# Block 2's projections on two alternating sets of PSUM banks, with the heads' norm sums after the next projection

## The chip, the cores and the metric

The kernel runs on one core of one Trainium2 chip. The metric is device time in microseconds (us) of one execution; lower is better.

## What is computed

Two transformer blocks on 512 tokens of width 1024, in float32. Block 1 is attention with a pooling mixer and a gated convolutional FFN. Block 2, which the change touches, starts with one wide projection, from which a neighbourhood attention and a two-way gated delta net are fed; a mixture of experts follows. The part of the reference that matters, cut:

```python
h = rms_norm(x, ln1_g)
proj = h @ w_in                          # (512, 3600)
aq, ak, av, dqkv, dz, dab = jnp.split(proj, [...], axis=-1)
aq = rms_norm(hs(aq), q_norm_g)          # per head of 64
ak = rms_norm(hs(ak), k_norm_g)
attn = rms_norm(neighbourhood_attention(aq, ak, hs(av), rpb), attn_out_g)
dn = bidirectional_gated_deltanet(dqkv, dz, dab[:, :, 0], dab[:, :, 1], conv_w, a_log, dt_bias, dn_out_g)
x = x + jnp.concatenate([attn, dn], axis=-1) @ w_out
x = x + hierarchical_moe(rms_norm(x, ln2_g), ...)
```

In the delta net q, k and v pass a depthwise convolution of width 5 and a SiLU; each chunk of its keys gives a triangular system that is solved.

## The kernel before

Every large product is made of float32 numbers split in two parts: `split_w` (L156) loads half a weight piece, ACT rounds it to `whi` (L170) and DVE makes the rest `wlo` (L171), each with three buffers. `proj` (L181) makes 256 output columns of all 512 tokens: two accumulators of 128 x 512, each one PSUM bank, and 3 x 8 matmuls for each (`mm3`, L177 to L179), 48 in all. The banks have tags (L102): `mm`, `pa` and `pb` have two each, `pc` and `gv` one.

```python
banks = dict(mm=2, pa=2, pb=2, pc=1, gv=1)
def proj(src, hh, hl, tag="mm", n=8):
```

In block 1's FFN the projections already take turns between tags (L619, L640). In block 2 all of them use `mm`, so the first matmul of one waits until ACT or DVE has read the banks of the one before. The value projections `na_v` make four tiles, one bank each, in turn in the two `mm` banks.

The stage is written in this order (L1208 to L1245): `na_q(0)`, the projection of the attention's keys, `na_v(0)`, `dn_k(0)`, `dn_k(1)`, `na_q(1)` (called q1 here), the keys' second projection (k1), `dn_q(1)`, `dn_q(0)`, `na_v(1)`, `substitute`, `dn_v(1)`, `dn_v(0)`, `dn_z(0)`, `dn_z(1)`, then `levels`, `scan_prep`, `na_pairs` and the scans. Each tile's waits are found by a planner, which also gives every engine a fixed queue: it goes by this order, but takes a later instruction when an earlier one isn't ready by its own estimate. A buffer or bank is given back when its last reader has run. Each engine works through its queue in order.

What the prediction follows:

- `head_norm` (L723): for each half of a projection ACT makes a gained copy `a` (L729) and a square `sq` (L732), both from the six buffers of tag `cv`; PE sums the squares of each head (`hn`, L735, 8 small matmuls for a half) into a `pa` bank; DVE (L739, L740, L743) and POOL (L742) make reciprocal roots. `head_rows` (L747) turns them into rows (`hr`, L750, a `pa` bank), which DVE copies to `hrow` (L752) and a DMA writes to `hscr` (L754). `head_bcast` (L757) reads them back into `hR`, and `na_q_out`, `na_k_out` (L769, L774) multiply the gained copies with them and thereby give these back.
- `conv_silu` (L863): ACT copies a projection's half out of its bank (`cn`, L866), POOL scales it (L867), ACT, DVE and ACT make the convolution and tanh (L868 to L874), DVE the result (L875). It holds two `cv` buffers from L866 to L875.
- `dn_k_out` (L957): for each head PE turns the keys (`ktr`, L961) and multiplies them (`kk`, L981), both in the one `gv` bank; `decay` (L942) makes E by DVE and ACT (L948), DVE makes U (L987), and DMAs write it out for `substitute`.
- `substitute` (L1004): 31 steps on DVE and POOL side by side (L1016, L1018) that need U of all four heads. `levels` (L1076) reads its result; its first matmuls are `lvY`.
- `na_pairs` (L796): the attention's logits `nS` (L812) go into `pa` banks, which DVE reads (L816); its sums `npo` use `pc`.

Of the kernel before, what the change touches and what calls it, by code (L numbers as in the profile page):

```python
# [14 lines left out]
AF = mybir.ActivationFunctionType  # L15
# [74 lines left out]
def hybrid_kernel(ctx, tc, A, out, dbg=None):  # L90
# [14 lines left out]
    def ps(tag, name):  # L105
        return pp.tile([128, 512], F32, tag=tag, name=name, bufs=banks[tag])
# [613 lines left out]
    nc.gpsimd.memset(vsh[0][0:64], 0.0)  # L720
    nc.gpsimd.memset(vsh[4][64:128], 0.0)

    def head_norm(pp, gain):  # L723

        pt = ps("pa", "hn")
        aa = []
        for m in range(2):
            a = slot("cv", "a", 6)
            nc.scalar.activation(a, pp[m], AF.Copy, scale=gain)  # L729
            aa.append(a)  # L730
            sq = slot("cv", "sq", 6)
            nc.scalar.activation(sq, pp[m], AF.Square)  # L732
            for t in range(4):
                o = m * 8 + t * 2
                nc.tensor.matmul(pt[:, o:o + 2], sq[:, t * 128:t * 128 + 128], C("hsel"), start=True, stop=True)  # L735
        v, r = (sp_.tile([128, 2] + d, F32, tag=f"hn{i}", name="hnv", bufs=1 + i) for i, d in enumerate(([4, 2], [2, 4])))
        pv = pt[:, 0:16].rearrange("p (m t e) -> p m t e", m=2, t=4)
        for m in range(2):
            nc.vector.tensor_tensor(v[:, m], pv[:, m], rr2.unsqueeze(2).to_broadcast([128, 4, 2]), op=ALU.mult)  # L739
        nc.vector.tensor_scalar(v, v, 1.0 / 64, EPS, op0=ALU.mult, op1=ALU.add)  # L740
        for m in range(2):
            nc.gpsimd.tensor_tensor(v[:, m], v[:, m], nhalf.rearrange("p (t e) -> p t e", t=4), op=ALU.pow)  # L742
            nc.vector.tensor_tensor(r[:, m].rearrange("p e t -> p t e"), v[:, m], rr.unsqueeze(2).to_broadcast([128, 4, 2]),  # L743
                                    op=ALU.mult)
        return aa, r

    def head_rows(aa, r):  # L747

        pr = ps("pa", "hr")
        nc.tensor.transpose(pr[0:16, 0:128], r.rearrange("p m e t -> p (m e t)"), ident)  # L750
        row = tmp("hrow")[0:16, 0:128]
        nc.vector.tensor_copy(row, pr[0:16, 0:128])  # L752
        hscr = drp.tile([2, 2, S], F32, tag="hscr", name="hscr", bufs=4)
        nc.sync.dma_start(hscr.rearrange("m e (t p) -> (m e t) p", t=4), row)  # L754
        return aa, hscr

    def head_bcast(hscr, m):  # L757
# [2 lines left out]
            nc.sync.dma_start(R[64 * e:64 * e + 64], hscr[m, e:e + 1].to_broadcast([64, S]))  # L760
        return R

    def na_q(c):
        return head_norm(proj(A["win2"][c] if c else w_first, hh, hl), g8)

    def na_q_out(c, aa, r):
        for m in range(2):
# [10 lines left out]
    def na_v(c):  # L778
        w = 256 if c else 272
        hi, lo = split_w(A["win2"][5] if c else A["win2v"], w=w)  # L780
        for i in range(4):
            p = ps("mm", "pv")
            ts = slice(i * 128, i * 128 + 128)
            for k in range(8):
                mm3(p[:, 0:w], hh[k][:, ts], hl[k][:, ts], hi[k], lo[k], k, k == 0, k == 7)
            if not c:
                nc.vector.tensor_scalar(dab[:, i, :], p[:, 256:272], rr[:, i:i + 1], None, op0=ALU.mult)
            v = slot("nP", "vn", 4, (128, 256))
            nc.scalar.activation(v, p[:, 0:256], AF.Copy, scale=rr[:, i:i + 1])
            nc.sync.dma_start(vscr[c][ts], v)  # L790
        src = vscr[c].rearrange("(r b x) w -> b r x w", r=8, b=8)
        for b in range(8):
            i, o = (b + 1) // 2, 64 * ((b + 1) % 2)
            nc.sync.dma_start(vsh[i][o:o + 64, c * 256:c * 256 + 256], src[b])
# [154 lines left out]
        E[d, h] = e  # L949

    def dn_k(c):
        p = proj(A["win2"][6 + c], hh, hl)
        for m in range(2):
            h = 2 * c + m
            conv_silu(p[m], 4 + h, kT[h])
# [66 lines left out]
                nc.sync.dma_start(xblk[d, h].rearrange("t b r c -> (t b) r c"), XB[i:i + 16])  # L1022

    def dn_q(c):
        p = proj(A["win2"][8 + c], hh, hl)
        for m in range(2):
            h = 2 * c + m
            conv_silu(p[m], h, qT[h])
# [11 lines left out]
    vT = {}  # L1040

    def dn_v(c):
        p = proj(A["win2"][10 + c], hh, hl)
        for m in range(2):
            h = 2 * c + m
            vT[h] = tmp("vT")
            conv_silu(p[m], 8 + h, vT[h])
# [12 lines left out]
    zs = []  # L1060

    def dn_z(c):
        p = proj(A["win2"][12 + c], hh, hl)
        z = slot("Z", "zs", 2, (128, 2, S))
        for m in range(2):
            zs.append(z[:, m])
            a = tmp("za")
            nc.vector.scalar_tensor_tensor(a, p[m], 0.5, RR, op0=ALU.mult, op1=ALU.mult)
            t = tmp("zt")
            nc.scalar.activation(t, a, AF.Tanh)  # L1070
            nc.vector.scalar_tensor_tensor(zs[2 * c + m], t, 1.0, a, op0=ALU.add, op1=ALU.mult)
# [135 lines left out]

    q_ = na_q(0)  # L1208
    x_rows(2)
    pk = proj(A["win2"][2], hh, hl)  # L1210
    x_rows(0)
    k_ = head_norm(pk, V("kg"))
    q_ = head_rows(*q_)
    na_v(0)
    x_rows(3)
    x_rows(1)
    na_q_out(0, *q_)
# [8 lines left out]
    na_k_out(0, *k_)  # L1226
    dn_k_out(0)
    q2_ = na_q(1)
    pk2 = proj(A["win2"][3], hh, hl)
    dn_k_out(1)  # L1230
    q2_ = head_rows(*q2_)
    na_q_out(1, *q2_)
    k2_ = head_norm(pk2, V("kg"))
    k2_ = head_rows(*k2_)
    na_k_out(1, *k2_)
    dn_q(1)
# [615 lines left out]
```

## Time and profile before

| | |
|---|---|
| median of three runs | 1566.13 us (1556.18 to 1568.72) |
| the profiled execution | 1565.13 us, span 1563.3 us |
| PE (TensorE) busy | 1472.4 us, 94% of the span |
| DVE (VectorE) busy | 835.6 us, 53% |
| ACT (ScalarE) busy | 516.3 us, 33% |
| POOL (GpSimd) busy | 248.3 us, 16% |
| mean granted TensorE clock | 0.969 |

All times of the trace are us from the start of the span. Block 2's projections run from about 625 to 856, the levels and scans to about 1000, the experts from 1074 to the end. A row of the timeline gives start, duration, engine, line, operation, output and inputs, how many instructions it merges, and in brackets how long the engine had been idle before and what ended that. Matmul ends are modelled and overlap the next starts. A clock of 1.00 is 2.4 GHz, and a mean between 0.50 and 1.00 in a stretch is a mix of 2.4 and 1.2 GHz.

### The profile page before, as it was taken

Reading aid. Unit: us, or ns where it says so; the run is one execution under the profiler, and the core shown is the slowest. Engines: PE = TensorE matmul, PEld = TensorE weight load, DVE = VectorE, ACT = ScalarE, POOL = GpSimd, SP = SyncE. Lnnn points to the kernel's source line nnn. Section 1 sums busy time; section 2 is a strip of 40 time slices with the busy share of each in tenths; the row PEclk is TensorE's granted clock in tenths of the full one; section 3 lists DMA queues with packets and bytes.
Section 4 is the critical chain, followed back from the end, with each engine's and each line's share of the span. In section 5 each row is a group of like instructions: output and inputs, shape, how many; then the busy total and the mean of one; then the engine's idle time right before and its main releaser. Section 6 shows DMA issues by size and latency. Waiting matters only on the chain.

```text
span 1563.3 us, 20383 instructions
## 1 busy us (share of the span) xinstructions
PE 1472.4 (94%) x7501; PEld 1009.8 (65%) x7501; DVE 835.6 (53%) x1665; ACT 516.3 (33%) x981; POOL 248.3 (16%) x314
## 2 busy tenths in 40 slices
PE   6989999999999999898889999997999999999997
PEld 2756687788888887786667788894444444444443
DVE  3669777654565467357797666635333333333234
ACT  3444434442333245354334444422311111111111
POOL 0234011000000003314471331102110000000000
PEclk8979999999999999998989999997999999999999
DMA  8664142322223223344243131567999999999995
GB/s 305 224 214 135 60 144 72 131 94 95 94 96 98 94 90 95 100 148 134 71 133 79 29 85 55 183 230 279 419 417 421 422 421 421 421 421 421 420 420 191
DMA packets 82573, 327.69 MB, mean 210 GB/s; under 512 B 18086, under 2 KB 21798, under 8 KB 58144
## 3 DMA queue, kind: packets, MB, share of 16 engines
q1 hardware_dynamic: 80736, 321.63, 55.3%
q0 software_dynamic: 1728, 4.66, 0.8%
q8 instruction: 61, 1.00, 0.3%
q14 instruction: 48, 0.39, 0.1%
HBM read 319.42 MB, written 8.47 MB: 210 GB/s over the span
## 4 chain that ended last, share of the span: by engine, by line
PE 75%; DVE 9%; DMA 6%; POOL 3%; issue 3%; ACT 3%; SPq 1%; DVEq 0%; POOLq 0%; ACTq 0%
PE pgu L1662 14%; PE pj L177 10%; PE pj L179 10%; PE pj L178 10%; PE pd L1691 7%; DMA graw<-in_modw_dram 3%; PE pkept L1709 2%; PE pkept L1710 2%; PE pcmb L1709 2%; PE pcmb L1710 2%; DVE wlo L171 1%; DVE cv L872 1%; DMA xg<-xs,tok_of 1%; PE pS L482 1%; PE po L178 1%
## 5 line engine op out<-in xcount | busy, mean ns | idle before, releaser
L177 PE MATMUL pj<-hh,whi 128*128 128x512 f32 x640 | 260.9, 409 | 18.7 <-ACT cn L866 8.5
L179 PE MATMUL pj<-hh,wlo 128*128 128x512 f32 x640 | 257.7, 404 | 2.4 <-DVE wlo L171 2.4
L178 PE MATMUL pj<-hl,whi 128*128 128x512 f32 x640 | 257.7, 403 | 0.6 <-DVE hl L200 0.6
L1662 PE MATMUL pgu<-wgu,xw 128*64 128x512 f32 x1024 | 226.8, 595 | 0.1
L171 DVE TENSOR_TENSOR wlo<-wraw,whi 128x1024 fp32r<-128x1024 f32 (+4 forms) x126 | 151.2, 1201 | 51.3 <-ACT whi L170 48.1
L170 ACT ACTIVATE whi<-wraw 128x1024 fp32r<-128x1024 f32 (+4 forms) x126 | 129.1, 1027 | 137.6 <-PE pj L178 115.8
L1662 PEld LDWEIGHTS pgu<-wgu,xw 128*64 128x64 f32 x1024 | 70.7, 137 | 139.0 <-issue 137.0
L177 PEld LDWEIGHTS pj<-hh,whi 128*128 128x128 f32 x640 | 123.9, 194 | 53.5 <-ACT cn L866 11.4
L179 PEld LDWEIGHTS pj<-hh,wlo 128*128 128x128 f32 x640 | 123.9, 194 | 32.6 <-issue 4.0
L178 PEld LDWEIGHTS pj<-hl,whi 128*128 128x128 f32 x640 | 123.9, 194 | 28.2 <-issue 2.1
L1668 DVE SCALAR_TENSOR_TENSOR hid<-pgu,agt,sg 128x256 f32<-128x256 f32 x32 | 15.5, 484 | 194.6 <-ACT sg L1666 194.6
L1666 ACT ACTIVATE sg<-pgu,agt 128x256 f32<-128x256 f32 x32 | 15.2, 474 | 306.9 <-PE pgu L1662 306.9
L1691 PE MATMUL pd<-wd,hT 128*64 128x512 f32 x512 | 115.5, 593 | 0.1
L1713 DVE TENSOR_TENSOR xr<-xr,pcmb 128x512 f32<-128x512 f32 x128 | 82.2, 683 | 30.3 <-PE pcmb L1710 30.3
L304 POOL TENSOR_TENSOR acc<-acc,sq 128x512 f32<-128x512 f32 x21 | 33.7, 1622 | 390.5 <-ACT sq L303 390.2
L198 DVE SCALAR_TENSOR_TENSOR og<-pd,agt,og 128x512 fp32r<-128x512 f32 x64 | 48.0, 751 | 79.5 <-ACT og L194 79.5
L1653 POOL COPY xw<-xgT 128x512 f32 x56 | 32.8, 614 | 356.0 <-PE pgu L1662 345.7
L1691 PEld LDWEIGHTS pd<-wd,hT 128*64 128x64 f32 x512 | 36.4, 137 | 71.9 <-issue 62.9
L179 PE MATMUL pj<-ah,wlo 128*128 128x512 f32 x176 | 69.3, 394 | 0.0
L177 PE MATMUL pj<-ah,whi 128*128 128x512 f32 x176 | 69.3, 394 | 0.0
L178 PE MATMUL pj<-al,whi 128*128 128x512 f32 x176 | 69.3, 394 | 0.0
L194 ACT ACTIVATE og<-pd,agt 128x512 fp32r<-128x512 f32 x64 | 44.0, 687 | 75.3 <-PE pd L1691 74.3
(454 smaller groups left out, 2607.1 us busy)
## 6 DMA issues: line engine op xcount, KB each, us to landing
wgu<-in_egu_dram SPq DMA_DIRECT2D x128, 1024.0 KB
wd<-in_ed_dram SPq DMA_DIRECT2D x62, 1024.0 KB
graw<-in_modw_dram SPq DMA_DIRECT2D x48, 512.0 KB
wraw<-in_wup_dram SPq DMA_DIRECT2D x42, 512.0 KB
wraw<-in_win_dram SPq DMA_DIRECT2D x38, 512.0 KB
wraw<-in_wdn_dram SPq DMA_DIRECT2D x20, 512.0 KB
wraw<-in_wout_dram SPq DMA_DIRECT2D x16, 512.0 KB
E<-gscr SPq DMA_DIRECT2D x16, 256.0 KB
```

Of the source, the lines that this page charges most:

```text
L170: nc.scalar.activation(hi, raw, AF.Copy)
L171: nc.vector.tensor_tensor(lo, raw, hi.bitcast(F32), op=ALU.subtract)
L177: nc.tensor.matmul(p, whi, hh, start=first, stop=False)
L178: nc.tensor.matmul(p, whi, hl, start=False, stop=False)
L179: nc.tensor.matmul(p, wlo, hh, start=False, stop=last)
L194: nc.scalar.activation(hi, src, AF.Identity, scale=scale, bias=0.0 if bias is None else bias)
L198: nc.vector.scalar_tensor_tensor(lo, src, scale, hi.bitcast(F32), op0=ALU.mult, op1=ALU.subtract)
L1662: nc.tensor.matmul(gu[64 * i:64 * i + 64, :], xw[:, j, 64 * i:64 * i + 64], wts.gu[e][j], start=(j == 0), stop=(j == 7))
L1691: nc.tensor.matmul(pd[64 * i:64 * i + 64, :], hT[:, j, 64 * i:64 * i + 64], wts.d[e][:, j, n * 512:n * 512 + 512], start=(j == 0), stop=(j ...
L1709: nc.tensor.matmul(pc, OT[:, ts], a, start=(n == 1 or start), stop=False, skip_group_check=(n == 0))
L1710: nc.tensor.matmul(pc, OT[:, ts], b, start=False, stop=(n == 1 or stop), skip_group_check=(n == 0))
L1713: nc.vector.tensor_tensor(v, v, pc, op=ALU.add)
```

## The change

Each projection of block 2 is given a tag, `mm` or `pa`, by a table `PJ`; consecutive ones differ, and the four value tiles alternate. `head_norm` is cut in two: `head_copies` makes the squares and gained copies (squares first) right behind the projection, and `head_norm` makes the sums later, behind the next projection (for the first keys: behind the value projection). Sums and rows move from `pa` to the single `pc` bank. The rows of the first q are made behind `na_v(0)` now.

```diff
--- before.py
+++ after.py
@@ -720,19 +720,23 @@
     nc.gpsimd.memset(vsh[0][0:64], 0.0)
     nc.gpsimd.memset(vsh[4][64:128], 0.0)
 
-    def head_norm(pp, gain):
-
-        pt = ps("pa", "hn")
-        aa = []
+    def head_copies(pp, gain):
+
+        aa, sqs = [], []
         for m in range(2):
-            a = slot("cv", "a", 6)
-            nc.scalar.activation(a, pp[m], AF.Copy, scale=gain)
-            aa.append(a)
-            sq = slot("cv", "sq", 6)
-            nc.scalar.activation(sq, pp[m], AF.Square)
+            sqs.append(slot("cv", "sq", 6))
+            nc.scalar.activation(sqs[m], pp[m], AF.Square)
+            aa.append(slot("cv", "a", 6))
+            nc.scalar.activation(aa[m], pp[m], AF.Copy, scale=gain)
+        return aa, sqs
+
+    def head_norm(aa, sqs):
+
+        pt = ps("pc", "hn")
+        for m in range(2):
             for t in range(4):
                 o = m * 8 + t * 2
-                nc.tensor.matmul(pt[:, o:o + 2], sq[:, t * 128:t * 128 + 128], C("hsel"), start=True, stop=True)
+                nc.tensor.matmul(pt[:, o:o + 2], sqs[m][:, t * 128:t * 128 + 128], C("hsel"), start=True, stop=True)
         v, r = (sp_.tile([128, 2] + d, F32, tag=f"hn{i}", name="hnv", bufs=1 + i) for i, d in enumerate(([4, 2], [2, 4])))
         pv = pt[:, 0:16].rearrange("p (m t e) -> p m t e", m=2, t=4)
         for m in range(2):
@@ -746,7 +750,7 @@
 
     def head_rows(aa, r):
 
-        pr = ps("pa", "hr")
+        pr = ps("pc", "hr")
         nc.tensor.transpose(pr[0:16, 0:128], r.rearrange("p m e t -> p (m e t)"), ident)
         row = tmp("hrow")[0:16, 0:128]
         nc.vector.tensor_copy(row, pr[0:16, 0:128])
@@ -760,8 +764,15 @@
             nc.sync.dma_start(R[64 * e:64 * e + 64], hscr[m, e:e + 1].to_broadcast([64, S]))
         return R
 
+
+    PJ = dict(q0="mm", k0="pa", v=("mm", "pa", "mm", "pa"), dk0="mm", dk1="pa", q1="mm", k1="pa", dq1="mm", dq0="pa",
+              dv1="mm", dv0="pa", dz0="mm", dz1="pa")
+
     def na_q(c):
-        return head_norm(proj(A["win2"][c] if c else w_first, hh, hl), g8)
+        return head_copies(proj(A["win2"][c] if c else w_first, hh, hl, tag=PJ[f"q{c}"]), g8)
+
+    def na_k(c):
+        return head_copies(proj(A["win2"][2 + c], hh, hl, tag=PJ[f"k{c}"]), V("kg"))
 
     def na_q_out(c, aa, r):
         for m in range(2):
@@ -779,7 +790,7 @@
         w = 256 if c else 272
         hi, lo = split_w(A["win2"][5] if c else A["win2v"], w=w)
         for i in range(4):
-            p = ps("mm", "pv")
+            p = ps(PJ["v"][i], "pv")
             ts = slice(i * 128, i * 128 + 128)
             for k in range(8):
                 mm3(p[:, 0:w], hh[k][:, ts], hl[k][:, ts], hi[k], lo[k], k, k == 0, k == 7)
@@ -949,7 +960,7 @@
         E[d, h] = e
 
     def dn_k(c):
-        p = proj(A["win2"][6 + c], hh, hl)
+        p = proj(A["win2"][6 + c], hh, hl, tag=PJ[f"dk{c}"])
         for m in range(2):
             h = 2 * c + m
             conv_silu(p[m], 4 + h, kT[h])
@@ -1022,7 +1033,7 @@
                 nc.sync.dma_start(xblk[d, h].rearrange("t b r c -> (t b) r c"), XB[i:i + 16])
 
     def dn_q(c):
-        p = proj(A["win2"][8 + c], hh, hl)
+        p = proj(A["win2"][8 + c], hh, hl, tag=PJ[f"dq{c}"])
         for m in range(2):
             h = 2 * c + m
             conv_silu(p[m], h, qT[h])
@@ -1040,7 +1051,7 @@
     vT = {}
 
     def dn_v(c):
-        p = proj(A["win2"][10 + c], hh, hl)
+        p = proj(A["win2"][10 + c], hh, hl, tag=PJ[f"dv{c}"])
         for m in range(2):
             h = 2 * c + m
             vT[h] = tmp("vT")
@@ -1060,7 +1071,7 @@
     zs = []
 
     def dn_z(c):
-        p = proj(A["win2"][12 + c], hh, hl)
+        p = proj(A["win2"][12 + c], hh, hl, tag=PJ[f"dz{c}"])
         z = slot("Z", "zs", 2, (128, 2, S))
         for m in range(2):
             zs.append(z[:, m])
@@ -1207,11 +1218,12 @@
 
     q_ = na_q(0)
     x_rows(2)
-    pk = proj(A["win2"][2], hh, hl)
+    k_ = na_k(0)
     x_rows(0)
-    k_ = head_norm(pk, V("kg"))
+    q_ = head_norm(*q_)
+    na_v(0)
     q_ = head_rows(*q_)
-    na_v(0)
+    k_ = head_norm(*k_)
     x_rows(3)
     x_rows(1)
     na_q_out(0, *q_)
@@ -1226,11 +1238,12 @@
     na_k_out(0, *k_)
     dn_k_out(0)
     q2_ = na_q(1)
-    pk2 = proj(A["win2"][3], hh, hl)
+    k2_ = na_k(1)
+    q2_ = head_norm(*q2_)
     dn_k_out(1)
     q2_ = head_rows(*q2_)
     na_q_out(1, *q2_)
-    k2_ = head_norm(pk2, V("kg"))
+    k2_ = head_norm(*k2_)
     k2_ = head_rows(*k2_)
     na_k_out(1, *k2_)
     dn_q(1)
```

## Rows read from the trace of the kernel before

**Rows 1.** Stretches: length; PE, PEld, DVE, ACT, POOL busy us (instructions); clock; DMA share; GB/s.

```profile
700.00:720.00 20.00, 14.35 (x68) 11.35 (x67) 19.57 (x33) 8.71 (x20) 10.80 (x9) 1.00 0.55 157
720.00:740.00 20.00, 18.81 (x77) 15.57 (x77) 11.99 (x39) 8.32 (x20) 6.84 (x13) 0.75 0.47 119
...
760.00:780.00 20.00, 14.46 (x70) 11.49 (x69) 15.34 (x41) 7.96 (x18) 8.06 (x21) 0.91 0.29 72
780.00:800.00 20.00, 14.34 (x94) 12.56 (x94) 17.14 (x33) 6.97 (x12) 17.88 (x30) 0.87 0.38 107
800.00:820.00 20.00, 17.55 (x68) 13.52 (x69) 19.41 (x45) 7.18 (x13) 12.80 (x18) 0.87 0.47 143
820.00:840.00 20.00, 18.37 (x83) 14.59 (x82) 19.98 (x46) 8.51 (x13) 4.38 (x5) 1.00 0.23 59
```

**Rows 2.** Whom PE waited for, 640 to 856: total us, times, longest.

```profile
PE pj L177 <- ACT cn L866: 8.5, 6, 4.5
PE hn L735 <- ACT sq L732: 5.6, 2, 5.2
PE pj L177 <- ACT vn L789: 2.9, 1, 2.9
...
PE pv L177 <- ACT cn L866: 1.7, 2, 0.9
...
PE pv L177 <- ACT vn L789: 1.5, 2, 0.9
```

**Rows 3.** A stretch of the FFN in block 1; columns as in rows 1.

```profile
300.00:360.00 60.00, 60.00 (x265) 49.42 (x264) 35.54 (x43) 24.62 (x32) 0.00 (x0) 1.00 0.31 99
```

**Rows 4.** PE in order of time, around k1.

```profile
720.84 1.87 PE L735 MATMUL hn<-cst,sq 128*128 128x2 f32 x8 [5.17 <-ACT sq L732]
...
729.97 0.67 PE L961 MATMUL ktr<-cst,kT 128*128 128x128 f32 x4
```

**Rows 5.** DVE in order of time, keys and substitution.

```profile
722.41 1.13 DVE L987 SCALAR_TENSOR_TENSOR U<-kk,nbrk,E 128x128 f32<-128x128 f32 x4
...
743.26 0.24 DVE L739 TENSOR_TENSOR hnv<-hn,rr 128x8 f32<-128x8 f32 x2 [3.90 <-PE hn L735]
743.42 1.12 DVE L987 SCALAR_TENSOR_TENSOR U<-kk,nbrk,E 128x128 f32<-128x128 f32 x4
...
771.73 0.24 DVE L752 COPY hrow<-hr 16x128 f32<-16x128 f32 x1
...
801.81 0.41 DVE L816 CUSTOM_DVE_ANT_0 nP<-nS,bm 128x256 f32<-128x256 f32 x1
...
836.54 0.15 DVE L1018 TENSOR_TENSOR XB<-XB,TB 128x8 f32<-128x8 f32 x1
```

**Rows 6.** ACT in order of time.

```profile
741.01 0.65 ACT L948 ACTIVATE E<-E 128x512 f32<-128x512 f32 x1
...
755.82 0.60 ACT L866 ACTIVATE cn<-pj 128x512 f32<-128x512 f32 x1 [1.71 <-PE pj L179]
...
767.48 0.60 ACT L866 ACTIVATE cn<-pj 128x512 f32<-128x512 f32 x1 [1.13 <-DVE qT L875]
```

**Rows 7.** PE in order of time, rows, logits, levels.

```profile
739.38 0.27 PE L750 MATMUL hr<-cst,hnv 128*16 128x128 f32 x1
...
775.16 0.70 PE L812 MATMUL nS<-akp,zq 64*128 64x256 f32 x2
...
855.99 1.06 PE L1095 MATMUL lvY<-DD,U 128*128 128x128 f32 x8
```

**Rows 8.** POOL in order of time, the substitution's start.

```profile
777.96 0.24 POOL L1016 TENSOR_TENSOR TB<-LB,XB 128x23 f32<-128x23 f32 x1
```

**Rows 9.** SyncE's queue, the first q's rows.

```profile
663.13 0.40 SPq L754 DMA_DIRECT2D hscr<-hrow  x1
...
686.90 2.43 SPq L760 DMA_DIRECT2D hR<-hscr  x4
```

**Rows 10.** PE's largest group from 1075: busy, mean ns, idle before.

```profile
L1662 PE MATMUL pgu<-wgu,xw 128*64 128x512 f32 x1022 | 226.3, 595 | 0.1
```

## Prediction

> **What bounds the kernel now.** The page's line of engines, in the table of time and profile above, comes first: PE has by far the largest share, so PE time saved is kernel time unless something else bounds the stretch where it is saved. Next the table of stretches for block 2's projections [rows 1]. Two things are to be seen in it: PE idles (14.35 us busy of 20 at 700, 14.46 at 760, 14.34 at 780), and its granted clock falls to 0.75, 0.91, 0.87 and 0.87 during or after such idleness; and VectorE (DVE) is full from 700 to 720 (19.57 of 20) and from 780 to 840 (17.14, 19.41, 19.98). So PE does not bound this stage alone. Third, whom PE waits for from 640 to 856 [rows 2]: ScalarE (ACT) copies that read a projection out of its banks: cn 8.5, sq 5.6, vn 2.9, and for the value projections 1.7 and 1.5, together 20.2 us. Fourth, a stage that already alternates its banks, the up projections of block 1's FFN [rows 3]: PE is busy 60.00 of 60 at clock 1.00, but DVE only 35.54 of 60. Last, PE, DVE and ACT in order of time, for what follows each wait [rows 4 to 8].
>
> **The change part by part.** *Banks.* No matmul is added or removed. Each projection gets another pair of banks than the one before it, so its first matmuls need not wait for that one's copies. On PE alone this removes at most the 20.2 us of [rows 2] and, with the idleness, the slow clock: (1-0.75) x 20 + (1-0.91) x 20 + 2 x (1-0.87) x 20 = 12.0 us [rows 1]. Upper bound 32.2 us; lower bound nothing, since the same copies can hold up something else.
>
> *What of it reaches the end.* The stage ends in a chain through the keys of the delta net's four heads: transposes ktr, copies, decay E, U (L987), the next head; then substitute, which needs every U; then levels. All heads' ktr and kk share the one gv bank, so head 1's ktr waits for head 0's last U, at 722.41 + 1.13 = 723.54 [rows 5]. It ran at 729.97 [rows 4]: on PE it stood behind q1's norm sums, which had waited 5.17 us for the squares, and behind the first matmuls of k1's projection at the slow clock. With k1's projection in its own banks and the sums behind it, PE goes straight on from 720.84 - 5.17 = 715.67 and can take ktr when the bank is free: 729.97 - 723.54 = 6.4 us. This is the main term. It is 0 if the new order puts another wait in front, and no more than 6.4, because U sets it.
>
> *The second wait on the chain.* Between two parts of head 1's U, DVE stood 3.90 us at hnv, for k1's norm sums [rows 5]. These now come 5.2 us of stall and some of the 5.0 us of slow clock earlier, so DVE should find them done. But U also needs its E from ACT, done at 741.01 + 0.65 = 741.66 [rows 6]: of the 3.90 us, 743.42 - 741.66 = 1.8 us are sure, and 3.4 us if ACT, which copied k1 ahead of that E, is free some 1.6 us earlier as well. I take 2.5, between the two.
>
> *After 778.* The substitution starts at 777.96 [rows 8], directly behind the last U, and its last step is at 836.54, 58.6 us later [rows 5]. From 780 to 840 DVE is busy 56.5 us of 60 [rows 1], so the end moves with the start and by no more than 3.5 us beyond it. I take 0: with more work ready at once, DVE fills, it doesn't shorten. The levels' first matmul, at 855.99 [rows 7], moves with it; PE, which ends its last projection just before, has more to spare than DVE.
>
> *Norm sums and squares.* The sums are only moved. A projection's two squares now stay in two of the six cv buffers until its sums have run, one projection later. So k1's second pair of copies waits for q1's sums (1.87 us for eight at the slow clock [rows 4]), which frees k1's banks some 2 us late, behind the next projection's 48 matmuls (48 x 60/265 = 10.9 us [rows 3]). They hide it: 0, and 2 us without them. Squares ahead of gained copies let sums start a copy earlier, which nothing waits for: 0. Pair 0's rows of q are now made behind the value projection: PE's one hr, DVE's hrow and SyncE's write of hscr pass that projection and its writes and reads on SyncE. That write was at 663.13, and the rows are read back at 686.90 [rows 9]; 23.4 us of slack hide the move, and behind them it would cost its own 0.40 us. POOL's powers move with the sums; POOL is busy 6.84 and 8.06 of 20 us at 720 and 760 [rows 1]: 0.
>
> *Sum.* 6.4 + 2.5 + 0 = 8.9 us. The profiled execution took 1565.13 us (span 1563.3 and 1.8 around it): 1565.1 - 8.9 = 1556.2. The median of the three runs lies 1.0 above that execution, within their spread of 12.5; I say 1556. The gain passes through to the end, as all that follows hangs on the levels and the experts' PE, once it runs, waits 0.1 us in 1022 matmuls [rows 10].
>
> **Two rules of the Trainium skill.** The FFN's alternating banks show a full PE [rows 3], block 2 shows 20.2 us of waits for banks [rows 2]. "Perfetto Trace Analysis", section Matmuls, says that independent groups of matmuls should rotate through different PSUM banks, so that one's evacuation overlaps the next one's matmuls; by that alone the sum would be the whole upper bound (the first rival). Against it speaks the same page's section Identifying the Most-Contended Engine: the engine with the highest occupancy is the one to improve. By that rule, from 780 on this is DVE and the change gives nothing. This trace agrees there, with 19.98 of 20, and not from 720 to 740, where DVE is busy 11.99.
>
> **The rivals.** *The banks give nearly everything.* For: the FFN's row; and DVE idles 8.0 us at 720 and 4.7 at 760 [rows 1], so it could take work earlier. Against: from 780 on it has 3.5 to give. PE's idle time at 700 and 760 goes (5.65 + 5.54 us), with the clock's loss at 720 and 760 (5.0 + 1.8), and 3.5 later: 21.5 us, 1544. The floor is 1565.1 - 32.2 = 1533.
>
> *DVE bounds it, no gain.* PE's stalls are hidden, because the copies that end them wait for buffers and not for banks. For: the copy at 767.48 waited for DVE's qT [rows 6], as gained copies of q1 and k1 hold four of the six cv buffers until their rows come back. Against: at 720 DVE itself waited, for PE. Then 1565, with DVE's slack of 3.5 to either side.
>
> *Slower: one bank for all norm sums.* The rows hr of q1 are turned at 739.38 [rows 7], but DVE copies them out only at 771.73 [rows 5]. Two pa banks let k1's sums pass them. In the single bank pc, if q1's hr gets in before k1's sums, these wait until 771.73 + 0.24 = 771.97; their squares keep two cv buffers, the gained copies four, and the next projection's first copy, today at 755.82 [rows 6], waits that long: 16.2 us on the convolutions, 1581. What decides is whether k1's squares are ready before q1's rows. The rows came 739.38 - 722.71 = 17 us after q1's first sums [rows 4, 7], the squares need only k1's last matmuls and copies of some 0.6 us each; so I hold it unlikely.
>
> *The logits keep the projections' banks.* The attention's first logits nS were issued at 775.16 [rows 7] into both pa banks, and DVE reads the first at 801.81 [rows 5], 26.7 us later. If that falls where projections want pa, PE has one projection of 10.9 us on the other set to put there: 15.8 us lost against 8.9 won, 1572.
>
> **How the numbers follow.** A measurement of this kernel can tell about 1% (15.7 us) from no change. Chances: the forecast 0.42, the banks give nearly everything 0.25, no gain 0.15, the logits 0.10, the single bank 0.08. A planner makes the order of the queues anew, which spreads each case by some us. The range 1538 to 1576 leaves out the single bank (0.08) and the lowest part of the first rival (about 0.10). The forecast's own range, each term between its bounds (0 to 6.4, 0 to 3.4, 0 to 3.5), is 1552 to 1565. Faster by over 1% (under 1549.5): the first rival and an edge of the forecast, 0.27. Slower by over 1%: the single bank and an edge of the logits, 0.10. Within 1%: 0.63.
>
> **What would show it.** Right: no wait of projections for cn, sq or vn above 1 us; head 1's ktr some 6 us nearer to q1's end; the clock near 1.00 where it was 0.75; the substitution starting near 769 and still about 58 us long; levels near 847. Wrong: a substitution much shorter than 58 us (the first rival), one that starts at 778 (no gain), k1's sums behind hrow (the single bank), or PE waiting at pj or pv for DVE's read of nS (the logits).

## The result, and the profile after

The changed kernel takes 1586.62 us (median of 4 runs, 1582.30 to 1590.90) against 1564.35 us beside it: a ratio of 1.014 [1.0111, 1.017], slower. The forecast was 1556.0 with a range of 1538 to 1576. The profiled execution took 1585.91 us, its span 1584.1.

One point before the rows are compared. Block 1 is the same code in both kernels, but its length differs from one execution to the next: the first matmul of row broadcasts (rb) in block 2's start, which the change doesn't touch, stands at 641.05 in the profile of before and at 634.91 in that of after. Below, "+x" is a time counted from that matmul in its own trace. So counted, the attention's last product (npo) ends at +351.2 before and at +376.6 after, and from there to the end it is 571 us in one and 573 in the other: nearly all that is lost is lost in these 370 us. So counted, equal code repeats closely: the first eight copies cn of before, e14 and e15 (two kernels of the experiments, whose code is that of before up to there) lie within 0.2 us of each other.

The stretches of after, with the columns of [rows 1]:

```profile
700.00:720.00 20.00, 16.00 (x72) 13.28 (x71) 17.78 (x39) 10.08 (x23) 6.87 (x16) 0.93 0.37 129
720.00:740.00 20.00, 17.80 (x92) 14.65 (x92) 11.13 (x47) 8.62 (x21) 7.88 (x14) 0.98 0.47 126
740.00:760.00 20.00, 17.46 (x87) 14.60 (x85) 13.10 (x43) 6.99 (x16) 4.49 (x18) 0.95 0.24 62
760.00:780.00 20.00, 12.37 (x66) 11.63 (x66) 9.82 (x21) 4.26 (x7) 12.20 (x15) 0.67 0.34 107
780.00:800.00 20.00, 9.90 (x47) 9.27 (x46) 9.62 (x15) 6.17 (x10) 18.12 (x29) 0.67 0.11 31
800.00:820.00 20.00, 19.04 (x70) 15.24 (x71) 15.08 (x36) 5.19 (x7) 7.32 (x12) 0.77 0.39 131
820.00:840.00 20.00, 19.15 (x84) 15.20 (x82) 18.06 (x38) 8.84 (x12) 5.39 (x3) 1.00 0.17 53
```

The stretch at 720 has a clock of 0.98 where it was 0.75, but it is not the same work: rb stands 6.14 us earlier in after. Counted from rb, the 20 us of before from 720 belong to these of after:

```profile
713.86:733.86 20.00, 15.42 (x76) 12.99 (x77) 12.17 (x44) 9.54 (x20) 7.66 (x17) 0.91 0.50 139
```

So the clock is better there, 0.91, and not full. And from 760 to 800 PE is busy 12.37 and 9.90 us of 20 at clock 0.67, and DVE, which was busy 17.14 of 20 at 780 [rows 1], is busy 9.62. Now PE, DVE and ACT idle together, which points to a chain that runs from queue to queue.

Whom PE waited for in after, 640 to 863 (total us, times, longest), against [rows 2]:

```profile
PE pv L177 <- ACT cn L877: 9.8, 2, 5.2
PE pqs L1047 <- ACT sq L1044: 4.9, 1, 4.9
PE hr L754 <- DVE hnv L747: 4.7, 2, 2.4
PE ktr L972 <- DVE U L998: 4.0, 1, 4.0
...
PE hn L739 <- DVE hrow L756: 2.5, 1, 2.5
```

No projection pj waits for a copy of cn or vn any more, and no sum hn for sq; the change does what it says. The value projection waits instead (pv for cn, 9.8 us where it was 1.7), and there is a short new wait, hn for hrow. It is only 2.5 us long, and it is the cause. PE, then ACT (k1's squares, sq, and what follows), in order of time:

```profile
725.87 1.84 PE L739 MATMUL hn<-cst,sq 128*128 128x2 f32 x16
731.87 0.27 PE L754 MATMUL hr<-cst,hnv 128*16 128x128 f32 x1 [2.20 <-DVE hnv L747]
757.49 2.97 PE L739 MATMUL hn<-cst,sq 128*128 128x2 f32 x16 [2.54 <-DVE hrow L756]
```

```profile
726.86 0.60 ACT L728 ACTIVATE sq<-pj 128x512 f32<-128x512 f32 x1 [0.30 <-PE hn L739]
...
758.78 0.60 ACT L877 ACTIVATE cn<-pj 128x512 f32<-128x512 f32 x1 [3.42 <-PE hn L739]
...
768.62 0.47 ACT L800 ACTIVATE vn<-pv,rr 128x256 f32<-128x256 f32 x1 [7.08 <-PE pv L179]
...
786.21 0.72 ACT L879 ACTIVATE cv<-cn,dcw 128x512 f32<-128x512 f32 x1 [8.62 <-POOL cn L878]
```

k1's squares are ready at 726.86 + 0.60 = 727.46. Their sums run at 757.49, 30 us later: q1's rows (hr, 731.87) were put into the single pc bank first, and DVE copies them out of it only at 757.19. The first copy of the next convolution (cn) waits for those sums, at 758.78, or +123.9; in [rows 6] it stood at 755.82, +114.8. DVE, POOL and SyncE show the rest:

```profile
755.40 1.12 DVE L998 SCALAR_TENSOR_TENSOR U<-kk,nbrk,E 128x128 f32<-128x128 f32 x4 [0.70 <-ACT E L959]
757.19 0.24 DVE L756 COPY hrow<-hr 16x128 f32<-16x128 f32 x1
...
786.97 0.75 DVE L883 SCALAR_TENSOR_TENSOR cv<-cn,dcw,cv 128x510 f32<-128x510 f32 x1 [8.39 <-ACT cv L879]
...
845.25 0.17 DVE L1029 TENSOR_TENSOR XB<-XB,TB 128x8 f32<-128x8 f32 x1
```

```profile
771.04 1.28 POOL L878 TENSOR_TENSOR cn<-cn,RR 128x512 f32<-128x512 f32 x1 [6.79 <-ACT cn L877]
772.28 0.23 POOL L1027 TENSOR_TENSOR TB<-LB,XB 128x23 f32<-128x23 f32 x1
...
784.50 0.46 POOL L1029 TENSOR_TENSOR XB<-XB,TB 128x140 f32<-128x140 f32 x1
784.92 1.26 POOL L878 TENSOR_TENSOR cn<-cn,RR 128x512 f32<-128x512 f32 x1
```

```profile
769.11 0.34 SPq L801 DMA_DIRECT2D vscr<-vn  x1
769.62 0.32 SPq L1009 DMA_DIRECT2D LB<-ublk  x1
```

Read them as one chain. The last U (755.40) is at hand, but the load of LB stands on SyncE behind the write of vn, which had to wait for a late value projection, and POOL stands at a late cn until 772.32; so the substitution starts at 772.28, +137.4, no earlier than in [rows 8] (777.96, +136.9). Which of the two came last, the load's landing or that cn, the trace doesn't tell. POOL then works through its steps of the substitution, and a late cn stands among them until 784.92; ACT's cv waits 8.62 us for that cn, DVE's convolution 8.39 us for that cv, and DVE's own steps of the substitution stand behind the convolution. Over the stretch DVE waits so for 18.8 us in five places, where before it was 5.4 in three (first after, then before):

```profile
DVE cv L883 <- ACT cv L879: 18.8, 5, 8.4
DVE cv L872 <- ACT cv L868: 5.4, 3, 2.9
```

From its first step to its last the substitution takes 845.25 - 772.28 = 73.0 us where it took 58.6 [rows 5, 8], and the levels begin at 863.16, +228.2, where they began at +214.9 [rows 7]. After that another 12 us is lost, for which the experiments are needed.

One more reading concerns the whole stretch from rb to the end of that last product, before and then after:

```profile
641.05:992.23 351.18, 318.85 (x1951) 265.75 (x1952) 232.43 (x581) 154.20 (x338) 116.59 (x156) 0.96 0.33 95
634.91:1011.53 376.62, 331.06 (x1956) 279.71 (x1956) 231.38 (x584) 155.18 (x339) 115.33 (x156) 0.91 0.30 89
```

PE does the same matmuls in it but for a few records. Of the 25.4 us, 13.2 are more idle time (45.6 us for 32.3), and 12.2 are more busy time for the same work, at a clock of 0.91 for 0.96. The lower clock has about as large a share in the loss as the waits.

### The profile page after: what moved, and what is told of

Read it like the earlier page. It is cut to its first block, busy times and chain, and to the rows that moved or that the text cites. A ratio compares the mean times of both kernels' runs of the same rounds, so it can differ in the third digit from the quotient of the medians.

```text
span 1584.1 us, 20378 instructions
## 1 busy us (share of the span) xinstructions
PE 1480.8 (93%) x7501; PEld 1023.2 (65%) x7501; DVE 833.5 (53%) x1665; ACT 516.0 (33%) x981; POOL 247.0 (16%) x314
## 4 chain that ended last, share of the span: by engine, by line
PE 76%; DVE 9%; DMA 5%; issue 4%; POOL 4%; ACT 2%; SPq 0%; DVEq 0%; POOLq 0%; ACTq 0%
PE pgu L1675 14%; PE pj L177 10%; PE pj L179 10%; PE pj L178 10%; PE pd L1704 7%; PE pkept L1722 2%; PE pkept L1723 2%; PE pcmb L1722 2%; PE pcmb L1723 2%; DMA graw<-in_modw_dram 1%; DVE wlo L171 1%; DMA xg<-xs,tok_of 1%; PE pS L482 1%; POOL TB L1027 1%; POOL XB L1029 1%
## 5 line engine op out<-in xcount | busy, mean ns | idle before, releaser
L177 PE MATMUL pj<-hh,whi 128*128 128x512 f32 x640 | 257.2, 403 | 7.1 <-DVE xT L643 3.3
L170 ACT ACTIVATE whi<-wraw 128x1024 fp32r<-128x1024 f32 (+4 forms) x126 | 129.1, 1027 | 133.8 <-PE pj L178 108.9
```

Of the source, the lines that this page charges most:

```text
L170: nc.scalar.activation(hi, raw, AF.Copy)
L177: nc.tensor.matmul(p, whi, hh, start=first, stop=False)
```

## The experiments

Two theories at first. A: the single bank pc costs the time, as k1's sums must wait in it for q1's rows. B: the projections that stand in pa take these banks from the attention's logits, whose work is then missing in PE's idle time ahead of the levels and is paid for behind them. A third, D, came up behind e7 and e9 and is in the expectations of e10 and e12: work ahead of the levels and behind them is zero-sum, as the logits' steps on VectorE delay the levels.

All kernels in one table. Columns: ratio to the kernel before beside it, with its 95% interval; then, from the one profiled execution of each kernel, the first cn of the second q projection's convolutions (cn), DVE's last step of the substitution (sub), the end of the last projection ahead of the levels (pj), the levels' first matmul (lvY), all as +x; then the stretch from there to the attention's last product, that product's end as +x, and how many nS matmuls stand ahead of the levels.

| kernel | ratio | cn | sub | pj | lvY | stretch | npo | nS |
|---|---|---|---|---|---|---|---|---|
| before | 1 | 114.8 | 195.6 | 214.7 | 214.9 | 136.2 | 351.2 | 12 |
| after | 1.0140 [1.0111, 1.0170] | 123.9 | 210.5 | 219.6 | 228.2 | 148.4 | 376.6 | 6 |
| e11_one_bank | 1.0149 [1.0105, 1.0192] | 127.7 | 215.4 | 230.9 | 232.5 | 141.6 | 374.1 | 12 |
| e8_sq_apart | 1.0063 [1.0038, 1.0089] | 108.8 | 185.9 | 203.1 | 204.4 | 152.3 | 356.7 | 0 |
| e2_sums_pb | 1.0041 [1.0016, 1.0067] | 112.3 | 185.4 | 204.9 | 206.1 | 154.8 | 361.0 | 0 |
| e1_all_mm | 1.0174 [1.0127, 1.0221] | 129.3 | 218.5 | 234.0 | 235.6 | 141.6 | 377.2 | 12 |
| e4_not_moved | 1.0127 [1.0102, 1.0152] | 126.7 | 210.6 | 218.1 | 224.8 | 149.5 | 374.3 | 2 |
| e5_moved_only | 1.0011 [0.9989, 1.0032] | 115.7 | 198.1 | 217.1 | 217.4 | 135.1 | 352.5 | 12 |
| e12_sets_only | 1.0051 [1.0027, 1.0076] | 114.5 | 188.6 | 206.0 | 207.3 | 153.5 | 360.8 | 0 |
| e3_pb_sets | 1.0113 [1.0082, 1.0145] | 119.1 | 209.1 | 216.1 | 226.8 | 144.3 | 371.1 | 12 |
| e7_early | 1.0079 [1.0052, 1.0107] | 112.4 | 204.5 | 220.5 | 221.4 | 139.8 | 361.2 | 16 |
| e9_early_not_moved | 1.0024 [1.0007, 1.0040] | 115.0 | 204.0 | 219.9 | 220.9 | 133.8 | 354.6 | 16 |
| e10_logits_mm | 1.0171 [1.0132, 1.0210] | 115.3 | 190.9 | 214.3 | 214.5 | 173.9 | 388.5 | 0 |
| e13_late_pb | 1.0030 [1.0009, 1.0051] | 112.6 | 194.8 | 204.6 | 207.0 | 147.7 | 354.7 | 12 |
| e14_less_pe | 1.0018 [0.9996, 1.0040] | 114.8 | 195.3 | 204.6 | 218.1 | 126.6 | 344.7 | 24 |
| e15_less_dve | 1.0008 [0.9995, 1.0021] | 114.7 | 184.9 | 213.3 | 213.6 | 137.9 | 351.5 | 12 |

**The bank undone in the changed kernel (e2_sums_pb).**

```diff
-        pt = ps("pc", "hn")
+        pt = ps("pb", "hn")
-        pr = ps("pc", "hr")
+        pr = ps("pb", "hr")
```

> Undoes the single bank alone: sums and rows go to the two pb banks, all else as in the changed kernel. Theory A: k1's sums no longer wait for hrow, the first convolution of dq1 starts near the end of its projection (about 748 instead of 759), total 1570 to 1578. Theory B: logits still lack pa, no logits before the levels, so total stays at 1582 to 1588.

1571.94 us. The two further banks give back some 16 of the 22 us, the substitution is short, and the levels begin 8.8 us earlier than before. What remains, 0.4%, comes behind the levels.

**The bank alone in the kernel before (e11_one_bank).**

```diff
-        pt = ps("pa", "hn")
+        pt = ps("pc", "hn")
-        pr = ps("pa", "hr")
+        pr = ps("pc", "hr")
```

> The kernel before with nothing of the change but the bank: the sums and their rows in the single pc bank, behind their own projection, all projections in mm. If the single bank is enough for the loss (theory A): the first copy of the second q projection's convolution starts 8 us or more later than before, and the time is 1578 to 1590 us. If it needs the alternation or the moved sums with it: 1562 to 1570 us.

1588.26 us: with nothing else of the change, the bank alone costs all of it. PE and ACT of this kernel show the same pair of waits, longer still:

```profile
738.37 0.27 PE L750 MATMUL hr<-cst,hnv 128*16 128x128 f32 x1
765.30 3.58 PE L735 MATMUL hn<-cst,sq 128*128 128x2 f32 x16 [9.21 <-DVE hrow L752]
```

```profile
767.21 0.60 ACT L866 ACTIVATE cn<-pj 128x512 f32<-128x512 f32 x1 [4.03 <-PE hn L735]
```

**The way by which the bank acts (e8_sq_apart).** The single bank stays; the squares leave the six cv buffers and take some of the tags hh and hl.

```diff
-            sqs.append(slot("cv", "sq", 6))
+            sqs.append(hp.tile([128, S], F32, tag=("hh", "hl")[m], name="sq", bufs=14))
```

> The changed kernel with its single pc bank, but the heads' squares are in buffers of their own instead of those that the convolutions take turns in. This tells by which way the single bank costs its time. If through the buffers (the squares of k1 are read late, so the first copy of the next convolution has no buffer until then): the copy that follows the first dq projection starts some 8 to 10 us earlier than in the changed kernel, the substitution on VectorE ends 15 us or more earlier, and the time comes down to 1568 to 1576 us. If through TensorE's own wait for the bank or the later rows of k1: no change, 1582 to 1590 us.

1572.14 us, as e2. Here k1's sums run even later than in the changed kernel, at +126.2 (after: +122.6), and it costs the convolutions nothing, because the convolution's copy no longer waits for them:

```profile
745.70 0.60 ACT L877 ACTIVATE cn<-pj 128x512 f32<-128x512 f32 x1 [1.73 <-PE pj L179]
```

So the loss is not PE's wait for the bank. It is that the late sums hold the squares, and the squares hold two of the six buffers that the convolutions need.

**The single bank with one other part undone.** e1_all_mm takes the alternation back, e4_not_moved the move of the sums.

```diff
-    PJ = dict(q0="mm", k0="pa", v=("mm", "pa", "mm", "pa"), dk0="mm", dk1="pa", ...
+    PJ = dict(q0="mm", k0="mm", v=("mm",) * 4, dk0="mm", dk1="mm", ...
```

> Undoes the alternation alone: all projections in mm again, sums still moved and in the single pc bank. Theory A (the single pc bank makes k1's sums wait for q1's hrow copy, so squares and gained copies fill the six cv buffers and the convolutions start late): the single bank stays, so most of the loss stays, 1578 to 1587 us. Theory B (projections in pa keep the attention's logits out of PE's idle time, which is then paid after the levels): pa is free for logits again, so the loss of the tail goes, 1565 to 1576, with logits before the levels' first matmul.

```diff
+    pk2 = proj(A["win2"][3], hh, hl, tag=PJ["k1"])
-    k2_ = na_k(1)
-    q2_ = head_norm(*q2_)
...
+    k2_ = head_norm(pk2, V("kg"))
-    k2_ = head_norm(*k2_)
```

> Undoes the move alone: sums right behind their own projection as before, squares behind gained copies, but alternation and the single pc bank kept. Theory A: k1's sums still share one bank with q1's rows, 1578 to 1587. Theory that the squares held through the next projection are the cause, not the bank: 1560 to 1570. Theory B: the logits still lack pa, so not under 1574.

1587.66 and 1585.54 us. With the one bank in place, neither other part matters: cn at +129.3 and +126.7, the substitution done at +218.5 and +210.6.

**The move alone (e5_moved_only).** The changed kernel with all projections in mm (as e1) and the sums in pa.

> The move of the norm sums alone: every projection in the two mm banks as before, the sums and their rows in the two pa banks as before, but the sums stand behind the next projection and the squares come ahead of the gained copies. If the single pc bank is the cause of the loss (theory A), the move by itself costs little: within 6 us of the kernel before (1560 to 1571 us), and the levels start within 5 us of before, counted from the first rb matmul. If the move itself is the cause (the squares stay in the convolutions' buffers through a projection and hold the convolutions up, whatever the bank), it shows 1575 us or more, and the first convolution of the second q projection starts some 9 us later than before.

1565.29 us, a ratio whose interval holds 1. The move and the squares' longer stay in the buffers are free, as the forecast had it, while the sums have two banks.

**The alternation alone (e12_sets_only).** The kernel before with the change's table of banks; sums behind their own projection, in pb.

```diff
-        pt = ps("pa", "hn")
+        pt = ps("pb", "hn")
-        pr = ps("pa", "hr")
+        pr = ps("pb", "hr")
-        p = proj(A["win2"][8 + c], hh, hl)
+        p = proj(A["win2"][8 + c], hh, hl, tag=PJ[f"dq{c}"])
```

> The alternation of the change in full and nothing else: sums behind their own projection, in pb's two banks. Theory D: no logits ahead of the levels, so as e2: levels 5 to 12 us earlier than before, a longer stretch behind them, 1567 to 1575 us. Theory of the prediction (the waits for the mm banks are the price): those waits are gone here too, and the time would be 1545 to 1558 us.

1572.43 us. This is the case that the forecast was about, freed of the bank. Its stretches from rb to the levels and from there to the last npo, and the same two of the kernel before (columns of [rows 1]):

```profile
638.70:845.99 207.29, 181.83 (x921) 152.86 (x922) 138.69 (x306) 83.98 (x153) 72.99 (x113) 0.93 0.41 117
845.99:999.54 153.55, 144.34 (x1035) 119.92 (x1035) 100.16 (x278) 71.36 (x188) 39.53 (x43) 0.96 0.21 60
```

```profile
641.05:855.99 214.94, 188.33 (x960) 155.19 (x960) 143.81 (x335) 92.24 (x179) 80.29 (x117) 0.94 0.38 110
855.99:992.23 136.24, 130.52 (x994) 110.57 (x993) 88.62 (x247) 61.96 (x159) 36.30 (x39) 0.99 0.26 72
```

The levels come 7.6 us earlier, but PE has done 39 matmuls fewer until then (921 records for 960; among them the attention's 12 nS, 6 nT and 8 npo, and 12 transposes vtr of the values), which is 6.5 us of busy time. Its idle time ahead of the levels is 25.5 us for 26.6: the waits that went have been replaced. One of the new ones is for weights (7.0 us in e2 as well), and pv waits 4.0 us for cn where it was 1.7:

```profile
PE pj L177 <- ACT whi L170: 7.1, 1, 7.1
```

The work left over stands behind the levels (1035 records for 994). Up to the last npo the two kernels do the same matmuls, and e12 needs 9.7 us more: 2.3 of idle time (34.7 for 32.3) and 7.3 of busy time (326.2 for 318.9), at a clock of 0.93 and 0.96 in the two stretches for 0.94 and 0.99.

**The alternation only early (e7_early, e9_early_not_moved).** k0, dk1, k1 and dq0 in pa, the later projections in mm, sums in pb; in e7 moved, in e9 not.

```diff
-    PJ = dict(q0="mm", k0="pa", v=("mm", "pa", "mm", "pa"), ..., dv0="pa", dz0="mm", dz1="pa")
+    PJ = dict(q0="mm", k0="pa", v=("mm",) * 4, ..., dv0="mm", dz0="mm", dz1="mm")
```

> As e2 (sums and rows in pb's two banks), but only the four projections k0, dk1, k1 and dq0 stand in pa; both value projections, dv0 and dz1 go back to mm, so that the pa banks are free for the attention's logits ahead of the levels. Theory B (in e2 the projections that stand in pa keep the logits out of the idle time ahead of the levels, and their work is paid for behind them): the levels start 5 to 9 us earlier than before, counted from the first rb matmul, the first logit is computed ahead of the levels as in the kernel before, and the time is 1553 to 1562 us. Rival: what e2 lost behind the levels has to do with the moved sums or the order on VectorE, not with the logits: then 1569 to 1575 us again, whether logits stand ahead of the levels or not.

> As e7 (k0, dk1, k1 and dq0 in pa, the other projections in mm, sums and rows in pb's two banks), but the sums stand behind their own projection as in the kernel before. If the alternation gives the gain and the move nothing: as e7 within 4 us. If the move is what keeps TensorE from waiting for the squares: 4 to 10 us slower than e7, with the second key projection's sums and kk products later.

1573.98 and 1567.16 us: B in its simple form falls. The logits do stand ahead of the levels again (16 nS in both), the stretch behind is about as short as before (139.8 and 133.8), but the levels now begin at +221.4 and +220.9, some 6 us later than before instead of 9 earlier. That e9 is better than e7 was in neither of its expectations, and why wasn't followed further.

**Other banks for the alternation (e3_pb_sets, e13_late_pb).** e3 alternates all projections between mm and pb with the sums in pa; e13 leaves the sums where they were and alternates with pb from dk1 on.

```diff
+    PJ = dict(q0="mm", k0="mm", v=("mm", "pb", "mm", "pb"), dk0="mm", dk1="pb", q1="mm", k1="pb", dq1="mm", dq0="pb",
+              dv1="mm", dv0="pb", dz0="mm", dz1="pb")
...
+            p = ps(PJ["v"][i] if c else "mm", "pv")
```

> The alternation kept, but between mm and pb; sums moved as in the changed kernel, but in the two pa banks. Both suspected costs go. Theories A and B together: 1552 to 1566, as forecast at first. If neither is the cause (the loss comes from the sums' place, or from the new order of the queues as such): 1578 to 1590.

> The kernel before, with sums and their rows where they were (behind their own projection, in pa), but the projections from dk1 on (k1, dk1, dq0, half of the second value projection, dv0, dz1) take turns between mm and pb; pa is left to the logits. Theory B (the alternation removes the waits for the mm banks and brings the levels forward by 6 to 10 us, as in e2, e8 and e12, and what it loses behind the levels is lost only because the logits have no bank ahead of them): levels at 205 to 210 us after the first rb matmul, with logits ahead of them, and 1553 to 1562 us. Rival (the earlier levels of e2, e8 and e12 and the logits ahead of them exclude each other, since both need the same time of TensorE and VectorE): levels at 213 us or later and 1562 to 1570 us.

1582.81 and 1568.46 us. e3 lies in the range that was set for neither A nor B. It doesn't decide between them, as it brings a delay of its own: the keys' chain is late from its first convolution (+51.9 against +47.7) on. Its early projections share pb with the transposes of block 2's input; that this is the reason wasn't shown. e13 is what B asked for: levels at +207.0, with as many logits ahead as before. Still the stretch behind them takes 11.5 us longer:

```profile
780.25:847.24 66.99, 58.98 (x264) 47.70 (x263) 57.69 (x123) 23.84 (x43) 34.54 (x50) 0.87 0.34 97
847.24:994.98 147.74, 136.90 (x1007) 114.99 (x1005) 98.26 (x261) 67.09 (x176) 37.95 (x41) 0.97 0.23 72
```

Of the 11.5 us, 6.4 are busy PE (136.90 against 130.52) and 5.1 idle; DVE has 9.6 us more to do there (98.26 against 88.62). Here too the levels' first matmul overtakes other work: 8 of the 16 vtr stand behind it, where before all 16 were ahead, and the last step of the two z projections (zs, L1071 in before) comes at +214.0 for +216.3, 2.3 us earlier and not 7.9. From rb to the last npo PE idles 31.7 us for 32.3, and is busy 323.0 for 318.9 with the same matmuls, so the 3.5 us that e13 loses there are busy time at a lower clock (0.95 for 0.96).

**The logits alone kept out (e10_logits_mm).** The kernel before, with nS and nT in the banks that the projections hold.

```diff
-            s = ps("pa", "nS")
+            s = ps("mm", "nS")
-                pt = ps("pa", "nT")
+                pt = ps("mm", "nT")
```

> The kernel before with nothing of the change; only the attention's logits and the transposed weights (nS, nT) take the two mm banks, which the projections hold until the last z projection, so no logits stand ahead of the levels. Theory D (work ahead of the levels and behind them is zero-sum: the logits' steps on VectorE delay the levels, the logits' steps on TensorE behind the levels delay the end): the levels start 5 to 12 us earlier than in the kernel before, counted from the first rb matmul, as in e2 and e8; the stretch from the first level to the attention's last product is 14 to 20 us longer; the time is 1567 to 1575 us. Rival: e2's and e8's earlier levels came from the banks or from the moved sums: then the levels start where they did before and the time is 1575 us or more.

1591.6 us. The levels stay at +214.5, and the stretch behind them grows by 37.7. So D falls in this form: logits ahead of the levels cost the levels of this kernel nothing, for without them PE idles 29.2 us there instead of 26.6. This trace is of the slowest of the five runs (1598.92), so the 37.7 may be some us too many. Part of the 37.7 may be that logits share mm with the levels of the second direction there; this wasn't taken apart. The rival's guess, 1575 or more, was the right one.

**What an engine's time ahead of the levels is worth (e14_less_pe, e15_less_dve).**

```diff
-        p = proj(A["win2"][12 + c], hh, hl)
+        p = proj(A["win2"][12 + c], hh, hl, use=1)
```

> The kernel before, with 84 of the 96 matmuls of the delta net's two z projections left out (seven of eight slices of the sum; their weights are still loaded and split, and all their copies are made). That takes 84 x 0.233 = 19.6 us from TensorE just ahead of the levels and nothing from the other engines: what the removal of bank waits could give at its best. If TensorE's time ahead of the levels sets the end: 15 us or more faster, 1549 us or less. If VectorE's order of work (substitution, convolutions, weight splits) sets it: less than 5 us faster, 1559 us or more.

```diff
-        for j in (0, 1, 3, 4):
+        for j in (0, 1, 3, 4) if ci < 8 else ():
```

> The kernel before, with the four outer taps of the four value convolutions left out: 16 steps of about 0.78 us on VectorE, 12.5 us, between the second value projection and the levels; TensorE's work is whole. If VectorE's time ahead of the levels sets the end: 8 us or more faster, 1556 us or less. If TensorE's does: less than 4 us faster, 1560 us or more.

1567.26 and 1564.23 us: 19.6 us less of PE and 12.5 us less of DVE each leave the time where it was. In e15 the substitution ends 10.7 us earlier, and the levels 1.3, since the last projection holds them (+213.3). In e14 the last projection ends 10.1 us earlier, and the levels come 3.2 us later: in PE's queue twice as many logits go ahead of them. So the levels' start in e14 says nothing of what else could hold them. The stretch behind is shorter, 126.6, and the attention ends 6.5 us earlier, a third of what was taken out. Even these 6.5 us don't arrive at the end. The stretch from 70 to 120 us behind the attention's last product, where the experts begin, of before and then of e14:

```profile
1062.20:1112.20 50.00, 44.72 (x232) 24.94 (x233) 20.07 (x55) 13.72 (x40) 9.89 (x10) 0.91 0.79 314
```

```profile
1050.90:1100.90 50.00, 39.45 (x187) 22.30 (x188) 19.92 (x75) 11.59 (x36) 8.02 (x8) 0.74 0.74 293
```

PE is busy 5.3 us less in it and at a lower clock. Whether that follows from the values that e14 leaves out (they feed the router) or from the earlier start wasn't tested.

## Why the prediction was wrong, step by step

**Banks: the named waits went, the idle time did not.** The waits of pj for cn and vn, and of hn for sq [rows 2], are gone in after, but pv waits 9.8 us for cn; the clock of the stretch at 720, counted from rb, is 0.91 for 0.75. In e12, without the single bank, PE's idle time ahead of the levels is 25.5 us for 26.6. And 5.6 of the 20.2 us, hn for sq, had been a wait for data and not for a bank.

**Head 1's ktr, 6.4 us: right.** It starts at 716.24, +81.3, for 729.97, +88.9 [rows 4], 7.6 us earlier. The norm sums in front of it run behind it, and it waits 4.0 us for U, as the step had it; that U ends 1.2 us earlier too.

**The second wait, 2.5 us: failed.** The last U starts at 755.40 and ends at +121.6, for +129.3 before: 7.7 us of the 8.9. But ktr alone brought 7.6 of them. From there to the end of the last U it takes 40.3 us, where it took 40.4. k1's sums no longer stand between the two parts of head 1's U (they come behind the last U, and that is the trouble itself), but the moved sums of q1 do, and DVE waits for POOL in them:

```profile
727.75 0.24 DVE L743 TENSOR_TENSOR hnv<-hn,rr 128x8 f32<-128x8 f32 x2 [0.59 <-PE hn L739]
...
731.55 0.17 DVE L747 TENSOR_TENSOR hnv<-hnv,rr 128x8 f32<-128x8 f32 x1 [1.43 <-POOL hnv L746]
731.64 1.12 DVE L998 SCALAR_TENSOR_TENSOR U<-kk,nbrk,E 128x128 f32<-128x128 f32 x4
```

**After 778, "0": failed.** The substitution was to start "directly behind the last U" and to last as long as before. Already before it stood 7.6 us behind the last U (+129.3 to +136.9). In after it started at +137.4, 16 us behind it, as its load had gone behind a late vn on SyncE and POOL was at a late cn; and it lasted 73.0 us. The step asked what fills DVE and not what DVE's queue waits for: in this trace the ready steps of the substitution stand behind a convolution that waits 8.39 us. The step had the path to the levels wrong as well: before, they begin 0.2 us behind the last projection (+214.7) and 19.3 behind the substitution (+195.6). In e13 12.2 us behind it are enough, and e15, with a substitution that ends 10.7 us earlier, moves the levels by 1.3.

**Norm sums and squares, "0", and the rival of the single bank at 0.08: the step that decided.** The rival named the place and the queue rightly. Its deciding point was wrong: "whether k1's squares are ready before q1's rows". They were, at 727.46 against 731.87, and it did not help. A bank is handed out in the order in which the code asks for it, and the code asks for q1's rows (`head_rows`) ahead of k1's sums (`head_norm`): no readiness lets the sums pass. That could be read in the diff; the traces agree, for in after, e1 and e8 k1's squares are ready first and its sums run behind hrow all the same. The 17 us between q1's sums and rows, taken from the old order, were 4.2 us in the new one (725.87 + 1.84 = 727.71 to 731.87). The price was mis-sized too: 16.2 us were forecast for the convolutions; the first cn came 9.1 us later than before (+123.9 for +114.8), and the queues behind made 13.3 us of it at the levels. e11 shows the bank alone to be enough, e8 the buffers to be its way.

**"The gain passes through to the end": failed, and would have failed without the bank.** In e2, e8 and e12 the levels come 8.8, 10.5 and 7.6 us earlier, near the forecast's 8.9, and the end is 0.4 to 0.6% later. The way is not the forecast's: the last U ends at +129.0, +124.7 and +132.2 in them, for +129.3 before, so clearly earlier in e8 alone. Nor is it saved idle time: in e12 6.5 of the 7.6 us are matmuls that PE has not done yet when the levels begin, and only 1.1 is less idle time. They are done behind the levels, where PE had 5.7 us of 136 to spare; the clock is lower besides, and 9.7 us are lost up to the last npo. The step took the levels' start for the end of the stage's work, and the waits of [rows 2] for idle time that nothing else would fill.

**The rivals.** "The banks give nearly everything" is refuted by e12, "no gain" comes nearest to what the change would be without the single bank (e2, 1.0041), and e12 shows what the logits' rival saw, by another way: the logits lose their banks to the projections, not the projections theirs to the logits.

**The two rules of the Trainium skill.** "Perfetto Trace Analysis", section Matmuls, on rotating banks: e12 rotates them, the waits of pj for cn and vn go, PE's idle time up to the last npo is 34.7 us for 32.3, and the time is 1.0051 [1.0027, 1.0076]. Its section Identifying the Most-Contended Engine would improve DVE in this stretch: e15 takes 12.5 us from DVE there for a ratio of 1.0008 [0.9995, 1.0021]. Here neither rule finds what holds the levels: in e15 they stand 0.3 us behind the last projection (+213.3).

**What stays open.** By what order of the queues PE's waits come back when the banks alternate, why the clock is lower in e12 and e13 at much the same idle time, why the early alternation with moved sums (e7) is slower than without (e9), and where e14's last 6.5 us go. No kernel here is faster than the one before.

## What to carry to other kernels

A shared bank is handed out in the order of the code and a queue is worked through in the planner's, so when two uses are put into one bank, write down that order and who must read the first before the second may start; here it was a copy on VectorE behind 25 us of other work. The length of a wait on the engine that waits says little of its price: 2.5 us at PE were the start of 13 at the levels, because the tiles that stayed occupied belonged to somebody else. And before a wait is costed as a gain, compare the engine's idle time up to a point where both kernels have done the same work: in e12 the waits for banks went, the levels began earlier, and TensorE had idled as long as before.

## What the runs showed of the hardware

One thing was not expected. The same instructions ahead of block 2 end at different times from one execution to the next: the first rb stands between 633.42 (e15) and 641.61 (e5), a spread of 8 us that is as large as the gain that was forecast. Single traces of this kernel can be compared only from a common instruction on.
